# The first 512 rows of a seven-product matmul: the second half of k as seven products instead of plain ones

## The chip, the cores and the metric

The kernel runs on one core of a Trainium2 chip. The metric is the device time of one execution in microseconds, and the median of several runs is compared. A profile of one execution gives the busy times of the engines: PE does matmuls, DVE and ACT do elementwise work, POOL and SP issue transfers (POOL those that turn fp32 into fp16 on the way, SP plain ones).

## The reference

```python
def setup_inputs():
    m, k, n = 4096, 4096, 4096
    return {
        "a": np.random.randn(m, k).astype(np.float32),
        "b": np.random.randn(k, n).astype(np.float32),
        "bias": np.random.randn(n).astype(np.float32),
    }

def reference(a: np.ndarray, b: np.ndarray, bias: np.ndarray) -> np.ndarray:
    return np.tanh(np.matmul(a, b) + bias)
```

## The kernel before

**Arithmetic.** a and b are turned to fp16 as they are loaded, and sums are kept in fp32 banks of 128 x 512 (there are eight). The columns of the output come in four chunks of 1024 (c = 0 to 3), each two banks wide. Rows come in pairs of 128-row blocks. For a pair and a chunk, a is seen as a 2 x 2 matrix of blocks (a11, a12, a21, a22: upper or lower row block, first or second of the two sets of k, 16 steps of 128 each) and b likewise. Seven products P1 to P7 take the place of eight (Strassen's scheme in Winograd's form): P1 = a11 b11, P2 = a12 b21, P7 = s3 t3, P6 = s2 t2, P5 = s1 t1, P3 = s4 b22, P4 = a22 t4, with the left sums s1 = a21 + a22, s2 = s1 - a11, s3 = a11 - a21, s4 = a12 - s2 and the right sums t1 = b12 - b11, t2 = b22 - t1, t3 = b22 - b12 (put over b12), t4 = b21 - t2. DVE makes these sums. One such product of one pair is 16 matmuls of 128 x 128 by 128 x 512, one per step of k. Two pairs are worked together and called a duo. Some products are done a second time in the same manner, on quarters ("fine", line 856 and `fine_product`, line 840).

**Work of one duo.** `work` (line 946) emits a product and what follows it. Two pairs have four kinds of banks, D, Z, I and C (line 854): P1 and P2 add in D, which is finished as the upper left output; after P1, Z gets a copy of D, and P6 adds to it; I takes P7, and its copy p7 is added to Z (`lift`) and, after P5, to C (`after_p5`, line 1025), which gives the lower right output; C begins as Z plus the difference of the biases (`after_p6`, line 1001), takes P5 and then P3 (upper right); P4 adds to Z (lower left). `run_duo` (line 1044) sets the order P1, P2, then P7, P6, P7, P6, P5, P5, then P3, P4, P4, and P3 of the second pair inside the next duo. When P3 is reached, s4 is made, over s2.

**The first stage** (lines 1946 to 2144) is another one. The rows 0 to 1023 (row blocks 0 to 7; `g0` are 0 to 3, `g1` are 4 to 7) by the first 1024 columns are done by plain matmuls, 32 steps of k each, while b's columns and these rows still arrive. 24 matmuls on zeros come first, ahead of any data (line 1965). The eight banks can hold four row blocks, so partial sums go out to fp32 buffers ("spill", by ACT) and are taken up again (by DVE): k's first part of g0, its first part of g1, the rest of g0's first half, g1 to the end, and at last g0's second half (line 2143: 128 matmuls). Each `finish` is tanh on ACT and a store on SP. The row blocks of a come by POOL (`land`, line 2002) and are transposed by DVE into 16 tiles `aq[m, h]` (row block m, h the set of k); the second half of k comes last, one row block at a time. Then `firsts` makes s1 and s2 of the pairs 0 and 1 for later, and stores (`keep`, line 594 does the transfer) put a11, a12, a22, s2 into scratch memory, since later chunks of columns need them again.

**After it**, the six duos of rows 1024 to 4095 do the first 1024 columns by seven products (line 2207), loading their rows as `nat` tiles by POOL; then come the other columns (`wide_pass` and the two passes, line 1572 and the fine products), with pieces of a fetched from scratch.

**What sets the order.** Every operation is put to a planner (`Plan`, line 159) with a duration, the buffers that it reads and writes, and its bytes. `rank` works out due times backwards from the end; `schedule` simulates engines, transfers and the places of the chip's memory (51, line 28) and emits the instructions of each engine in the order of that simulation. A big buffer takes one place, an "out" buffer half of one. A transfer waits until its buffer has a place. `soft` brings a due time near that of what comes before it, `after` adds an operation that must precede; that is an order in the plan and no wait on the chip, unless a buffer is shared. Lines that the change touches besides: `load_bias` (line 913) and `store` and `finish` (lines 484 and 491), `product` (line 825), whose matmuls read the whole of a left tile as far as the planner knows.

The lines that set the end of the first stage:

```python
    for m, j in swapped:
        down(4 + m, j, 2 * T - TB, 2 * T, stop=True)
        finish(mb(m, j), 4 + m, j * NB)
        take_up(m, j, k0)
    for m, j in swapped:
        down(m, j, T, 2 * T, stop=True)
        finish(mb(m, j), m, j * NB)
```

Of the kernel before, what the change touches and what calls it, by code (L numbers as in the profile page):

```python
# [18 lines left out]
G = 2  # L19
WARM = 24  # L20
fp32 = mybir.dt.float32
# [137 lines left out]
class Plan:  # L159
# [14 lines left out]
    def add(self, eng, dur, emit, reads=(), writes=(), nbytes=0, hw=True, soft=None, early=0.0, lead=0.0, reach=1e9, after=None, long=False):  # L174
# [6 lines left out]
        if nbytes:  # L181
            kind = ("POOL", "LONG")[long] if not hw else "out" if soft is not None else "in"
            rate, wait = RATES[self.open][kind]
            op.flow, op.wait = nbytes / (rate * SPEED), wait + SLACK
            op.share = SHARES[self.open][long]
            op.kind = 0 if soft is None else 2 if writes else 1
# [222 lines left out]
def kernel(  # L409
# [73 lines left out]

    def store(o, row, col, n):
        add(
            "SP", 0.34,
            lambda: nc.sync.dma_start(out=out[ds(row * P, P), ds(col, n)], in_=o[ALL]),
            (o,), (), nbytes=P * n * 4, soft=1.0,
        )

    def finish(src, row, col):

        o = new("o", [P, NB], fp32, "out")
        act(NB, lambda: nc.scalar.activation(o[ALL], src[ALL], TANH), (src,), (o,), soft=2.0)  # L494
        store(o, row, col, NB)

# [328 lines left out]
    def product(bank, left, right, t0, nt, start=False, shift=0):  # L825

        for k in range(t0, t0 + nt, TB):
            rb = right[k // TB]

            def emit(k=k, rb=rb):  # L830
                for t in range(TB):
                    nc.tensor.matmul(  # L832
                        bank[ALL], left_tile(left, k + t + shift), rb.tile(t),
                        start=start and k == t0 and t == 0, stop=k + t == t0 + nt - 1,
                        skip_group_check=True,
                    )

            add("PE", TB * 0.2158, emit, ((left, left.atoms), *rb.deps()), (bank,))

# [73 lines left out]
    def load_bias(c, after=None):  # L913
        k = {}
        k["b1"] = new("bias", [P, 2, NB], fp32, atoms=2)
        src = bias[ds(c * NCW, NCW)]
        add(
            "SP", 0.34,
# [3 lines left out]
            ),  # L922
            (), (k["b1"],), nbytes=P * NCW * 4, after=after,
        )
# [18 lines left out]
    class Duo:  # L943
        pass

    def work(duo, name, s, part=None, last=True):
# [48 lines left out]
    def after_p1(d, s, part):  # L995
        if d.x == 0:
            src, atom = (d.k["b1"], 0) if part != 1 else (d.box[s], 0)
# [1119 lines left out]
    for m, j in rows4:  # L2117
        down(4 + m, j, 0, TB, True)
    across(g1, TB, TP - 2)
    for m, j in rows4:  # L2120
        down(4 + m, j, TP - 2, TP, stop=True)
        put_aside(4 + m, j)
        take_up(m, j)
    k0 = load_bias(0, plan.last_pe)
    for m, j in rows4:
        down(m, j, TB, TP)
    across(g0, TP, T - 2)
    for m, j in rows4:
        down(m, j, T - 2, T, stop=True)
        if j == 0:  # L2130
            new_spill(m)
        put_aside(m, j)
        take_up(4 + m, j, k0)
    for m, j in rows4:
        down(4 + m, j, TP, T)
# [9 lines left out]
    firsts = {}  # L2145
    for p in FIRST:
        s = {f"a{r + 1}{h + 1}": aq[2 * p + r, h] for r in range(2) for h in range(2)}
        asum(s, "s1", "a21", "a22", ADD, soft=2.0)
        asum(s, "s2", "s1", "a11", SUB, over="s1", soft=2.0)
        firsts[p] = s  # L2150
        if not KEEP_AT[p]:
            keep(p, s)
    finish_bias(k0)
    for blk in range(4):
        bsums(bop, blk)

    plan.open = 1
    stored |= early if TWO == 1 else set(range(NP))  # L2160
    k, before, held = k0, None, None
    for c in range(NC):
# [44 lines left out]
        for i, pairs in enumerate(duos):  # L2207
# [28 lines left out]
            for p in FIRST if c == 0 else ():  # L2236
                if KEEP_AT[p] == i + 1:
                    keep(p, firsts[p], after=plan.last_pe)
    def place_tile(buf):
# [44 lines left out]
```

## Time and profile before

| what | value |
|---|---|
| time, median of 3 runs | 1432.6 us (1432.56 to 1432.8) |
| time of the profiled execution | 1433.78 us |
| its span, first to last instruction | 1432.1 us |
| bytes moved by DMA | 399.19 MB |
| granted PE clock, mean | 1.000 |
| plain matmuls of the first stage (line 2049) | 512, from 9.80 us on |

In the rows of a timeline the columns are start and duration in us, engine, line, operation, output <- inputs, count, and in brackets the idle time ahead of it and what ended it. PEld is the loading of weights for PE, POOLq and SPq are the issue of transfers. A name like a or s is that of a buffer without its number; `parts` is a shared place of smaller buffers. In a view of waits the columns are total, times and longest in us. In a view of groups they are count, busy us, mean ns of one, and idle time before. In the DMA view a queue has packets, MB and a share (q0 is POOL's, q1 SP's), and a transfer has its count, KB and median us from issue to landing.

### The profile page before, as it was taken

Reading aid. Unit: us, or ns where it says so; the run is one execution under the profiler, and the core shown is the slowest. Engines: PE = TensorE matmul, PEld = TensorE weight load, DVE = VectorE, ACT = ScalarE, POOL = GpSimd, SP = SyncE. Lnnn points to the kernel's source line nnn. Section 1 sums busy time; section 2 is a strip of 40 time slices with the busy share of each in tenths; the row PEclk is TensorE's granted clock in tenths of the full one; section 3 lists DMA queues with packets and bytes.
Section 4 is the critical chain, followed back from the end, with each engine's and each line's share of the span. In section 5 each row is a group of like instructions: output and inputs, shape, how many; then the busy total and the mean of one; then the engine's idle time right before and its main releaser. Section 6 shows DMA issues by size and latency. Waiting matters only on the chain.

```text
span 1432.1 us, 22563 instructions
## 1 busy us (share of the span) xinstructions
PE 1422.2 (99%) x8408; PEld 822.2 (57%) x8408; DVE 1078.1 (75%) x1594; ACT 392.8 (27%) x746; POOL 325.3 (23%) x613
## 2 busy tenths in 40 slices
PE   9999999999999999999999999999999999999998
PEld 4444555555644444444444444444447888888887
DVE  3359968767985376796568787988798689997876
ACT  3111212221333333311111133233233332244433
POOL 8764332334452341100111130000130300000000
PEclk9999999999999999999999999999999999999999
DMA  9999998899999899997899799899999987788883
GB/s 188 178 236 286 251 293 196 222 240 221 274 276 316 235 274 302 280 358 290 265 291 294 270 294 389 341 367 344 334 335 354 271 248 265 250 297 286 304 301 134
DMA packets 167486, 399.19 MB, mean 279 GB/s; under 512 B 25425, under 2 KB 44369, under 8 KB 167377
## 3 DMA queue, kind: packets, MB, share of 16 engines
q1 hardware_dynamic: 104400, 318.03, 61.2%
q0 software_dynamic: 62976, 79.73, 33.4%
q8 instruction: 66, 1.08, 0.3%
q14 instruction: 44, 0.35, 0.1%
HBM read 327.68 MB, written 149.68 MB: 333 GB/s over the span
## 4 chain that ended last, share of the span: by engine, by line
PE 76%; DMA 2%; DVE 1%; POOL 0%; issue 0%; ACT 0%; SPq 0%; DVEq 0%
PE ps L1572 45%; PE ps L847 25%; PE ps L832 6%; DMA nat<-in_a_dram 1%; DMA xa<-a 1%; DMA s<-a 1%; DVE a L473 0%; POOL nat L530 0%; DVE s L473 0%; DVE a L506 0%; DVE u L473 0%; ACT parts L1370 0%; DVE ys L473 0%; DVE parts L473 0%; DVE za L684 0%
## 5 line engine op out<-in xcount | busy, mean ns | idle before, releaser
L759 POOL DMA_DIRECT2D b<-in_b_dram x320 | 169.7, 535 | 607.7 <-DMA out_dram<-u 163.6
L476 ACT COPY ps<-ps 128x256 f32<-128x256 f32 (+1 forms) x216 | 100.8, 467 | 443.0 <-PE ps L1572 306.0
L530 POOL DMA_DIRECT2D nat<-in_a_dram x224 | 118.5, 533 | 208.8 <-DMA nat<-in_a_dram 51.6
L473 DVE TENSOR_TENSOR u<-ps,u 128x512 f32<-128x512 f32 x160 | 106.1, 686 | 26.2 <-PE ps L1572 25.1
L473 DVE TENSOR_TENSOR parts<-ps,parts 128x512 f32<-128x512 f32 (+1 forms) x129 | 72.6, 563 | 67.2 <-PE ps L1572 40.0
L832 PEld LDWEIGHTS <-a 128*128 128x128 f16 x704 | 68.8, 98 | 81.9 <-issue 2.4
L473 DVE TENSOR_TENSOR ps<-ps,parts 128x256 f32<-128x256 f32 (+1 forms) x151 | 82.7, 552 | 39.4 <-PE ps L1572 22.0
L2049 PE MATMUL ps<-b,o 128*128 128x512 f16 x512 | 111.3, 379 | 0.1
L476 ACT COPY parts<-ps 128x256 f32<-128x256 f32 (+1 forms) x151 | 69.0, 461 | 135.9 <-DVE ps L473 45.6
L1572 PE MATMUL ps<-b,zs 128*128 128x512 f16 x448 | 105.8, 379 | 0.0
L1572 PEld LDWEIGHTS <-ya 128*128 128x128 f16 x624 | 61.1, 98 | 73.6
L506 DVE STREAM_TRANSPOSE a<-nat 128x512 uint32<-128x512 uint32 x112 | 73.2, 690 | 20.8 <-DMA nat<-in_a_dram 17.4
L832 PE MATMUL ps<-b,a 128*128 128x512 f16 x384 | 84.7, 379 | 2.1 <-DVE parts L473 2.1
L1572 PEld LDWEIGHTS <-zs 128*128 128x128 f16 x512 | 50.1, 98 | 60.2
L1572 PEld LDWEIGHTS <-xa 128*128 128x128 f16 x512 | 50.1, 98 | 60.2
L2049 PEld LDWEIGHTS <-o 128*128 128x128 f16 x512 | 49.8, 98 | 60.3 <-ACT o L2094 0.5
L494 ACT ACTIVATE parts<-ps 128x512 f32<-128x512 f32 x52 | 31.0, 597 | 162.4 <-PE ps L832 98.1
L1572 PE MATMUL ps<-b,za 128*128 128x512 f16 x320 | 75.6, 379 | 0.0
L473 DVE TENSOR_TENSOR b<-b,b 128x2048 f16<-128x2048 f16 (+2 forms) x76 | 68.0, 910 | 10.1 <-DMA b<-in_b_dram 9.5
L832 PE MATMUL ps<-t,a 128*128 128x512 f16 x320 | 72.3, 379 | 0.0
L1572 PEld LDWEIGHTS <-za 128*128 128x128 f16 x384 | 37.6, 98 | 45.3
L847 PEld LDWEIGHTS <-ya 128*128 128x128 f16 x592 | 57.9, 98 | 7.1
(163 smaller groups left out, 2560.1 us busy)
## 6 DMA issues: line engine op xcount, KB each, us to landing
b<-in_b_dram POOLq DMA_DIRECT2D x320, 128.0 KB, 8.0
ya<-a SPq DMA_DIRECT2D x70, 512.0 KB, 7.2
xa<-a SPq DMA_DIRECT2D x70, 512.0 KB, 7.2
u<-U SPq DMA_DIRECT2D x62, 512.0 KB, 6.6
nat<-in_a_dram POOLq DMA_DIRECT2D x224, 128.0 KB, 8.0
U<-u SPq DMA_DIRECT2D x48, 512.0 KB, 6.9
ys<-s SPq DMA_DIRECT2D x46, 512.0 KB, 5.0
xs<-s SPq DMA_DIRECT2D x46, 512.0 KB, 5.6
```

The lines of the kernel that those rows point to most:

```text
L473: dve(n, lambda: nc.vector.tensor_tensor(out=o(), in0=x(), in1=y(), op=op), reads, writes, wide, **kw)
L476: act(n, lambda: nc.scalar.copy(o(), x()), reads, writes, **kw)
L494: act(NB, lambda: nc.scalar.activation(o[ALL], src[ALL], TANH), (src,), (o,), soft=2.0)
L506: nc.vector.transpose(dst[ALL].rearrange("P t m -> P (t m)").bitcast(pair32).rearrange("P (U m) -> P U m", m=P)[:, ds(t0 // 2, nu), ds(row ...
L530: nc.gpsimd.dma_start(out=tl[(ds(q * QP, QP), *key)], in_=src)
L759: nc.gpsimd.dma_start(out=dst.rearrange("p t j n -> p t (j n)") if j is None else dst, in_=src)
L832: nc.tensor.matmul(bank[ALL], left_tile(left, k + t + shift), rb.tile(t), start=start and k == t0 and t == 0, stop=k + t == t0 + nt - 1, s ...
L847: nc.tensor.matmul(bank[ALL, HALF[half]], left_tile(buf, at_ * TP + i * TB + t), rb.tile(t), start=False, stop=i == 1 and t == TB - 1, ski ...
L1572: nc.tensor.matmul(bank[ALL, cols], left_tile(buf, at_ * TP + i * TB + t), rb.tile(t, half), start=start and not (i or t), stop=i == 1 and ...
L2049: nc.tensor.matmul(bank[ALL], left_tile(left, t), rb.tile(tb), start=start, stop=stop, skip_group_check=True,)
```

## The change

The first 512 rows keep plain matmuls only for the first half of k (`CLASSIC` = 16 steps). Their plain sums U = [u11 u12; u21 u22] (upper and lower row block, left and right bank) stay in the spill buffers, with the bias added. The second half of k is then done as a duo of its own by `run_duo`, each product over 8 steps, 14 products. The plain sums are fed in so that each output receives its own: D starts as u11 (an ACT copy) and Z is copied from it, I starts as u22's part less u12 (DVE), C gets e = u12 - u11 after P6, and Z gets one more sum at the lift. The left sums s1, s2, s3, s4 are made in halves of k, so that the first half need not wait for the second.

Beside that: s4 goes over a12 instead of s2 in all later duos of these columns (`S4_OVER`); the bias load now follows a DVE memset of its buffer that is ordered behind a matmul, and so waits on the chip; the stores of rows 512 to 1023 are put behind the store of row block 3's second tile (`behind`), and that store is pulled forward; the warm-up has 18 matmuls; the right sums are made for the blocks 1, 2, 3, 0 in place of 0 to 3; stores to scratch of the pairs 0 and 1 have other due times.

```diff
-WARM = 24
+WARM = 18
+CLASSIC = 16
+LATE_STORES = 2
+SLACK_OPEN = 0.8
+S4_OVER = 'a12'
-WARM_TIME = 7.6
+WARM_TIME = 6.7
...
+            rows_of = left.atoms if t0 == 0 else (k // TB,) if len(left.atoms) == 4 else (k // TP,)
-            add("PE", TB * 0.2158, emit, ((left, left.atoms), *rb.deps()), (bank,))
+            add("PE", TB * 0.2158, emit, ((left, rows_of), *rb.deps()), (bank,))
...
+        if after:
+            dve(NH, lambda: nc.vector.memset(k["b1"][ALL, 0, HI], 0.0), (), (k["b1"],), after=after)
...
         if name == "P3" and "s4" not in a_:
-            asum(a_, "s4", "a12", "s2", SUB, over=None if d.stays else "s2")
+            if d.sums:
+                d.last_sum(a_)
+            else:
+                asum(a_, "s4", "a12", "s2", SUB, over=None if d.stays else S4_OVER)
...
+        if d.sums:
+            t0, nt, start = CLASSIC // 2, T - CLASSIC // 2, False
...
+        elif d.sums:
+            e = d.sums[s]
+            tt(at(C[s]), at(Z[s]), at(e), ADD, NB, (Z[s], e), (C[s],))
...
+            if d.sums:
+                low = spill[d.pairs[s] * 2 + 1]
+                tt(at(Z[s]), at(Z[s]), at(low, ALL, 0), ADD, NB, (Z[s], (low, (0,))), (Z[s],))
...
     for m, j in rows4:
-        down(m, j, T - 2, T, stop=True)
-        if j == 0:
-            new_spill(m)
+        down(m, j, T - 2 if CLASSIC == T else TB, CLASSIC, stop=True)
         put_aside(m, j)
         take_up(4 + m, j, k0)
...
+    for m in g0:
+        tt(at(spill[m]), at(spill[m]), at(k0["b1"]), ADD, 2 * NB, (spill[m], k0["b1"]), (spill[m],))
+    first_duo = Duo()
+    d = first_duo
+    d.sums = []
+    for s in range(2):
+        up, low = spill[2 * s], spill[2 * s + 1]
+        e = new("e", [P, NB], fp32, "out")
+        tt(at(e), at(up, ALL, 1), at(up, ALL, 0), SUB, NB, (up,), (e,))
+        tt(at(low, ALL, 0), at(low, ALL, 0), at(low, ALL, 1), SUB, NB, (low,), ((low, (0,)),))
+        tt(at(low, ALL, 0), at(low, ALL, 0), at(e), ADD, NB, ((low, (0,)), e), ((low, (0,)),))
+        d.sums.append(e)
+    behind = None
+    if LATE_STORES:
+        m = 2 * LATE_STORES - 1
+        early_row = {"a22": aq[m, 1]}
+        keep(LATE_STORES - 1, early_row, ("a22",), soft=1.0)
+        behind = plan.ops[-1]
     for m, j in swapped:
         down(4 + m, j, 2 * T - TB, 2 * T, stop=True)
-        finish(mb(m, j), 4 + m, j * NB)
-        take_up(m, j, k0)
-    for m, j in swapped:
-        down(m, j, T, 2 * T, stop=True)
-        finish(mb(m, j), m, j * NB)
+        finish(mb(m, j), 4 + m, j * NB, behind)
+    for s in range(2):
+        copy(at(D[s]), at(spill[2 * s], ALL, 0), NB, ((spill[2 * s], (0,)),), (D[s],))
+    for s in range(2):
+        up, low = spill[2 * s], spill[2 * s + 1]
+        tt(at(I[s]), at(low, ALL, 1), at(up, ALL, 1), SUB, NB, ((low, (1,)), (up, (1,))), (I[s],))
+    finish_bias(k0)
+    for blk in (1, 2, 3, 0):
+        bsums(bop, blk)
...
+    for p in FIRST:
+        half_sum(s, "s1", "a21", "a22", ADD)
+        half_sum(s, "s3", "a11", "a21", SUB, over="a21")
+        half_sum(s, "s2", "s1", "a11", SUB)
...
+    d.c, d.k, d.bop, d.pairs = 0, k0, bop, list(FIRST)
+    d.x, d.next, d.put = 0, STEEP[0][0], ()
+    before = run_duo(d, None)
```

More of the change, by code (lines that the diff above doesn't have):

```diff
@@ L183, in add @@
             rate, wait = RATES[self.open][kind]
-            op.flow, op.wait = nbytes / (rate * SPEED), wait + SLACK
+            op.flow, op.wait = nbytes / (rate * SPEED), wait + (SLACK if self.open else SLACK_OPEN)
             op.share = SHARES[self.open][long]
@@ L482, with store @@
     ALL = slice(None)
-    def store(o, row, col, n):
+    def store(o, row, col, n, after=None):
         add(
@@ L943 @@
     class Duo:
-        pass
+        sums = None
     def work(duo, name, s, part=None, last=True):
@@ L995, in after_p1 @@
     def after_p1(d, s, part):
-        if d.x == 0:
+        if d.x == 0 and not d.sums:
             src, atom = (d.k["b1"], 0) if part != 1 else (d.box[s], 0)
@@ new lines, with half_sum, atoms @@
+    for s in range(2):
[6 more added lines that the diff above has]
+        bsums(bop, blk)
+    def half_sum(s, name, x, y, op, over=None, halves=(0, 1)):
+        x, y = s[x], s[y]
+        if name not in s:
+            s[name] = s[over] if over else new(name, [P, T, P], atoms=2)
+        def atoms(v, h):
+            return (h,) if len(v.atoms) == 2 else (2 * h, 2 * h + 1)
+        for h in halves:
+            key = ALL, ds(h * TP, TP)
+            tt(
+                at(s[name], *key), at(x, *key), at(y, *key), op, TP * P,
+                ((x, atoms(x, h)), (y, atoms(y, h))), ((s[name], atoms(s[name], h)),), wide=False,
+            )
@@ L2145, with last_sum @@
+    def last_sum(s):
+        half_sum(s, "s4", "a12", "s2", SUB, over="s3", halves=(1,) if CLASSIC == T else (0, 1))
     firsts = {}
+    d.a, d.last_sum = [], last_sum
     for p in FIRST:
         s = {f"a{r + 1}{h + 1}": aq[2 * p + r, h] for r in range(2) for h in range(2)}
-        asum(s, "s1", "a21", "a22", ADD, soft=2.0)
-        asum(s, "s2", "s1", "a11", SUB, over="s1", soft=2.0)
+        half_sum(s, "s1", "a21", "a22", ADD)
+        half_sum(s, "s3", "a11", "a21", SUB, over="a21")
+        half_sum(s, "s2", "s1", "a11", SUB)
@@ L2150 @@
         firsts[p] = s
+        d.a.append(s)
         if not KEEP_AT[p]:
[L2152 to L2155, printed above, removed]
+            keep(p, s, [n for n in BASIS if n != "a22" or p != LATE_STORES - 1], soft=3.0)
+    d.c, d.k, d.bop, d.pairs = 0, k0, bop, list(FIRST)
+    d.x, d.next, d.put = 0, STEEP[0][0], ()
+    d.parts = d.last = d.stays = False
+    before = run_duo(d, None)
     plan.open = 1
     stored |= early if TWO == 1 else set(range(NP))
-    k, before, held = k0, None, None
+    k, held = k0, None
@@ L2237 @@
                 if KEEP_AT[p] == i + 1:
-                    keep(p, firsts[p], after=plan.last_pe)
+                    keep(p, firsts[p], [n for n in BASIS if n != "a22" or p != LATE_STORES - 1], after=plan.last_pe, soft=3.0)
     def place_tile(buf):
```

21 lines of the change are left out of this document (12 added, 9 removed).

## The prediction

> **What bounds the kernel now.** I read the page first, then the view of waits for PE, PE's timeline and the chain of waits.
>
> ```profile
> span 1432.1 us, 22563 instructions
> PE 1422.2 (99%) x8408; PEld 822.2 (57%) x8408; DVE 1078.1 (75%) x1594; ACT 392.8 (27%) x746; POOL 325.3 (23%) x613
> ```
>
> ```profile
> PE ps L832 <- DVE parts L473: 2.1, 1, 2.1
> PE ps L847 <- DVE a L473: 1.7, 1, 1.7
> ...
> PE ps L847 <- ACT ps L476: 0.4, 1, 0.4
> ```
>
> PE is busy in 1422.2 of 1432.1 us, and in the whole run it stands still for another engine only three times (in the columns: total, times, longest), together 4.2 us. So a matmul that goes is worth its own time, a wait that goes is worth its own, and nothing else can pay.
>
> ```profile
> 11.18 110.11 PE L2049 MATMUL ps<-b,o 128*128 128x512 f16 x508
> 121.12 13.98 PE L832 MATMUL ps<-b,a 128*128 128x512 f16 x64
> ...
> 141.84 3.62 PE L832 MATMUL ps<-b,s 128*128 128x512 f16 x16
> ```
>
> The first stage runs without a gap. One matmul ends 0.38 us after its start, so the second row gives (13.98 - 0.38) / 63 = 0.216 us from one to the next.
>
> ```profile
> 409.53 189.95 PE ps L1572 x880
> ...
> 599.76 1.35 POOL nat L530 x3
> ...
> 637.58 440.47 PE ps L1572 x2040
> ```
>
> Where the chain leaves PE, at 599.5 us, POOL takes up right behind a PE instruction that freed a place, so that detour moves with PE: what is won before 600 us should arrive at the end.
>
> **The change part by part.**
>
> **A, the products.** The last 128 plain matmuls (512 rows, 1024 columns, 16 steps of k) become 14 products of 8 matmuls, 112. Sixteen go: 16 x 0.216 = **-3.5 us**, on PE's own path.
>
> **B, the start.** Six of 24 warm-up matmuls go, and the bias load no longer stands first on SP's queue.
>
> ```profile
> 1.40 7.63 PE L1968 MATMUL warm<-zeros 128*128 128x512 f16 x24 [1.40 <-DVE zeros L1962]
> ```
>
> ```profile
> 9.35 0.26 PEld L2088 LDWEIGHTS <-first 128*128 128x128 f16 x4 [0.24 <-DMA first<-in_a_dram]
> ...
> 10.86 0.27 PEld L2088 LDWEIGHTS <-first 128*128 128x128 f16 x4 [0.28 <-DMA first<-in_a_dram]
> ```
>
> ```profile
> 6.12 0.77 POOL L1975 DMA_DIRECT2D first<-in_a_dram  x1
> ```
>
> ```profile
> DMA to landing us min/median/max: 4.3/4.8/5.0
> ```
>
> The warm-up ends later than the first tile, but the second and the fourth tile of a's first columns are waited for, and the fourth was issued at 6.12 and landed 4.8 us on, at 10.9. Six matmuls at 0.216 are 1.3 us, and that is the upper end. As the loads hold PE back anyway, the gain is what a queue without the bias brings the fourth tile: from nothing to 10.86 - (6.12 + 4.3) = 0.4. I take **-0.2**. The same bias load now falls among loads that are late in the stage; that price is in D.
>
> **C, s4 in a12's place.** This touches every later duo of the first 1024 columns.
>
> ```profile
> 234.46 6.55 SPq L594 DMA_DIRECT2D s<-a  x3
> ```
>
> ```profile
> 250.45 1.23 DVE L473 TENSOR_TENSOR a<-a,a 128x2048 f16<-128x2048 f16 x1 [4.55 <-DMA s<-a]
> 251.59 0.68 DVE L473 TENSOR_TENSOR parts<-ps,parts 128x512 f32<-128x512 f32 x1
> ...
> 272.53 1.30 DVE L506 STREAM_TRANSPOSE a<-nat 128x512 uint32<-128x512 uint32 x2 [2.73 <-DMA nat<-in_a_dram]
> ...
> 279.75 1.23 DVE L473 TENSOR_TENSOR a<-a,a 128x2048 f16<-128x2048 f16 x1
> ```
>
> ```profile
> 252.33 3.61 PE L832 MATMUL ps<-b,a 128*128 128x512 f16 x16 [2.11 <-DVE parts L473]
> ...
> 281.04 1.05 PE L847 MATMUL ps<-b,a 128*128 128x256 f16 x8 [1.71 <-DVE a L473]
> ```
>
> ```profile
> 254.78 4.20 POOL L530 DMA_DIRECT2D nat<-in_a_dram  x8 [9.62 <-DVE parts L473]
> ```
>
> The reader is to see one cause behind two of the three waits. At 245.9 DVE comes to s4 = a12 - s2, which goes over s2, and s2 is still being stored to scratch (issued from 234.46 on). DVE's queue is in order, so for 4.55 us everything behind stands too: first the sum that empties bank C, for which PE waits 2.11 us, then the op whose end frees a place for POOL's next eight loads of a. Those are late, DVE waits for them at 272.53, and PE at 281.04 waits 1.71 for the DVE op that follows. With s4 over a12, whose store is earlier, there is nothing to wait for: 2.11 + 1.71 = **-3.8 us**. Ends: 0 (another store takes its place) and -3.8.
>
> **D, the new junction.** P1 of the first duo would start at 121.12 - 128 x 0.216 = 93.5, less B 93.3. Products are half as long, 1.73 us. What must be there by then:
>
> ```profile
> 88.42 2.52 POOL L530 DMA_DIRECT2D land<-in_a_dram  x4 [0.52 <-DMA land<-in_a_dram]
> ...
> 127.66 0.53 POOL L530 DMA_DIRECT2D nat<-in_a_dram  x1 [0.66 <-DMA nat<-in_a_dram]
> ```
>
> ```profile
> 88.28 0.70 DVE L473 TENSOR_TENSOR ps<-spill,bias 128x512 f32<-128x512 f32 x1 [26.00 <-ACT parts L494]
> ...
> 101.27 1.30 DVE L506 STREAM_TRANSPOSE o<-land 128x512 uint32<-128x512 uint32 x2
> ```
>
> ```profile
> q0 software_dynamic: 1871, 2.38, 111.8%
> ...
> land<-in_a_dram POOLq DMA_DIRECT2D x12, 128.0 KB, 5.4
> ```
>
> ```profile
> q0 software_dynamic: 1324, 1.21, 82.2%
> ```
>
> ```profile
> q0 software_dynamic: 1418, 2.32, 61.9%
> ...
> nat<-in_a_dram POOLq DMA_DIRECT2D x18, 128.0 KB, 9.0
> ```
>
> The three q0 rows are POOL's bytes in 75 to 88, 88 to 97 and 110 to 130 us: 183, 134 and 116 KB/us. The drop at 88 comes with the stores of rows 512 to 1023. Now these stores stand on SP behind the store of a row block of a that lands among the last, so until then POOL keeps 183: 9 x (183 - 134) = 0.44 MB earlier, 3.8 us at 116. Against this the bias (0.5 MB) now falls into the stage: 0.5 / 0.183 = 2.8 us at worst, nothing if it shares. The last row block (issued from 88.42 to 90.94) then lands at 90.94 + 5.4 = 96.3, transposed 1.3 later, against 101.9 before. P1 and P2 want rows 0 and 2, and the due times put those first; rows 1 and 3 are wanted from P7 on, at 93.3 + 32 x 0.216 = 100.2. So the loads of this stage should do. The next duo's last load is issued at 127.66, lands 9.0 later, and needs two transposes (1.3) and a sum (1.2): 139.2, where P7 of its second half started at 141.84 and now would at 138.2. It is 1.0 late if its loads do not come earlier, and on time if a third of those 3.8 us stays.
>
> ```profile
> L473 DVE TENSOR_TENSOR ps<-spill,bias 128x512 f32<-128x512 f32 x16 | 10.4, 684 | 28.4 <-ACT parts L494 26.0 <-ACT spill L476 2.4
> ...
> L473 DVE TENSOR_TENSOR t<-b 128x1024 f16<-128x1024 f16 x8 | 5.1, 686 | 0.0
> ...
> L473 DVE TENSOR_TENSOR s<-o,o 128x2048 f16<-128x2048 f16 x2 | 2.4, 1210 | 0.0
> ```
>
> DVE's work: the bias on four spills (8 x 0.68 = 5.5, no row has the whole width), six sums of halves (4.1), bank I (1.4), eight sums behind P6, P7, P5 (5.5), 16 half sums of a (16 x 0.64 = 10.2); gone are eight sums that took up rows 0 to 511 (5.5) and four whole sums (4.8). Net +16.4 us. Of it the spills (9.6) and the lower half sums (3.8) need nothing later than 62 us and lie in the 26.0 us in which DVE stood idle; cover gone, they are 13.4 us in front of P7. The rest, 3 us, is in a stretch where DVE has no pause. There a product behind a DVE sum has 1.73 us where it had 3.45: own 0.68 plus one 1.21 us sum ahead is 1.9, with a transpose too 2.6. Three places have such a turn (P6 to P5, P5 to P3, P7 to P4), 0.2 to 0.9 each. I take 0.5 each: **+1.5 us**; ends 0 and 6.9 (below). The ACT copies added (six) lie on an engine busy in 27% of the span.
>
> The Trainium skill speaks here (DMA: Bandwidth & Descriptors, section Queues, rings and completion order): each engine goes round robin, packet by packet, between the queue rows that have work. By that rule a store held back costs the loads nothing later, since a longer row takes no larger share, and the 3.8 us stay; the sum is as here. Were it shared by waiting bytes instead, they would be given back by 110 us, and D would be 2.5, the time 1428.1. The drop from 183 to 134 agrees with sharing by turns, but does not show what a longer row does.
>
> **E, the rest.** Every place is laid out anew behind the first stage. PE waits 0.4 us there, so nothing is to be won: 0 to +3, I take **+0.5**.
>
> **Sum:** -3.5 - 0.2 - 3.8 + 1.5 + 0.5 = -5.5. The profiled run took 1433.8 us, of which 1432.1 are the span; the median of the runs is 1432.6, 1.2 less than that run. The three become 1428.3, 1426.6 and **1427.1**.
>
> **Rivals.**
>
> *All clean:* A, B, C without D and E, -7.5: **1425.1**. For it: DVE's idle 26 us, the loads' 3.8 us. Against: turns of 1.73 us on an engine without a pause.
>
> *The operands are late:* rows 2's block stays last, as in the rows above, and is transposed at 101.27 plus 0.65 for its first half, 101.9; P1 of the second half wants it at 95.0. PE waits 6.9: **1432.0**. For it: DMA is full until then. Against: due times and stores held back.
>
> *The change does not do what it says:* s4 waits for a12's store, or o = C + p7 is late for another reason. C is 0: **1430.9**. Against: a12's store is issued with the row, s2's only after all sums.
>
> *Slower, by places:* s2 used to carry s4 to the end; now a12's place stays to the end of P3 and s2's until its store has landed.
>
> ```profile
> POOL nat L530 <- DVE a L506: 20.1, 3, 10.0
> ```
>
> ```profile
> 219.69 10.52 PE L832 MATMUL ps<-b,a 128*128 128x512 f16 x48
> ...
> 259.24 1.04 PE L847 MATMUL ps<-b,a 128*128 128x256 f16 x8
> ```
>
> ```profile
> 234.02 4.20 POOL L530 DMA_DIRECT2D nat<-in_a_dram  x8 [6.13 <-PE ps L847]
> ```
>
> P2 ends at 230.0 and let go of a12; two places are now held until about 250.4, when s2's store had landed. POOL waits for places already, three times behind transposes alone. If the eight loads of 234.02 had to start at 250.45, they would land 9.0 us later, and with a transpose (0.65) and four half sums (2.6) the fine P1 would start at 262.7 instead of 259.24: 3.4 late. With C lost and three such duos, -3.7 + 10.2: **1439.1**. It decides from 1.3 us a duo on. Against: places are shared, and two of the kernel's 51 are at stake.
>
> **Numbers.** Forecast 1427.1 (1425.6 to 1429.7): 0.50. All clean: 0.13. Operands late, 1432.0: 0.14. C missing, 1430.9: 0.09. Slower by places: 0.14. About 0.2% (2.9 us) is what a measurement of this kernel tells from no change: faster is below 1429.7, slower above 1435.5. Faster 0.50 + 0.13 + 0.02 (the lower part of the case without C) = 0.65; same 0.21; slower 0.14. The range leaves out half of the clean case's tail below 1424.6 (B at its 0.4 and more) and the case by places: 1424.6 to 1434.0.
>
> **What would show it.** A: 112 matmuls at the line of the products between the last plain one and the next duo. B: the first plain matmul near 9.6. C: no DVE wait for a store of s near 250, and none of PE at 252 and 281. D: PE's waits at the products' line between 93 and 142. E: no PE wait behind 282 that is not there now. The forecast is wrong if PE stands more than 4 us in D's stretch, or if POOL's loads of a in the next duos start later relative to PE than now.

## The result, and the profile after

| | before | after |
|---|---|---|
| median, same chip (21 runs each) | 1433.78 us | 1431.41 us |
| lowest to highest | 1432.29 to 1437.43 | 1427.62 to 1434.46 |
| profiled execution, its span | 1433.78, 1432.1 us | 1431.41, 1429.1 us |
| mean granted PE clock of that execution | 1.000 | 0.998 |
| runs at a mean granted clock of 1.000 (full speed) | (26 of 35 in a second set) | 6 of 21 |

The ratio is 0.9983, interval 0.9975 to 0.9990: 2.4 us faster (1.4 to 3.6), where 5.5 were forecast. The direction held and the time lies in the range; less than half of the gain arrived.

The head of the page of the kernel after:

```profile
span 1429.1 us, 22558 instructions
...
PE 1417.6 (99%) x8386; PEld 820.4 (57%) x8386; DVE 1090.6 (76%) x1617; ACT 395.6 (28%) x752; POOL 325.4 (23%) x613
```

PE has 4.6 us less work. That is 1.1 more than the 16 matmuls of step A: six warm-up matmuls went too, and the start gave some back. The span shrank by 3.0 only. The view of waits for PE (total, times, longest) shows where the rest is:

```profile
PE ps L852 <- DVE a L477: 2.8, 1, 2.8
PE tp L2106 <- DMA first<-in_a_dram: 2.7, 1, 2.7
...
PE ps L852 <- DVE ps L477: 0.3, 1, 0.3
PE ps L852 <- ACT ps L480: 0.2, 1, 0.2
```

Before there were waits of 2.1 and 1.7 at two places of the later duos. Now there is one of 2.8, and a new one of 2.7 at the start, ahead of the transposes of a's second tile. PE's timeline of the kernel after (its lines stand 4 to 18 further down: 836 is the line of the products, 852 of the fine ones, 2067 of the plain matmuls) puts them in their places:

```profile
1.40 5.43 PE L1986 MATMUL warm<-zeros 128*128 128x512 f16 x18 [1.40 <-DVE zeros L1980]
6.67 0.39 PE L2106 MATMUL tp<-ident,first 128*128 128x128 f16 x4
9.78 0.41 PE L2106 MATMUL tp<-ident,first 128*128 128x128 f16 x4 [2.72 <-DMA first<-in_a_dram]
...
11.82 83.49 PE L2067 MATMUL ps<-b,o 128*128 128x512 f16 x380
95.14 8.80 PE L836 MATMUL ps<-b,o 128*128 128x512 f16 x40
...
133.13 3.62 PE L836 MATMUL ps<-b,s 128*128 128x512 f16 x16
...
248.44 3.62 PE L836 MATMUL ps<-b,a 128*128 128x512 f16 x16
...
278.24 1.05 PE L852 MATMUL ps<-b,a 128*128 128x256 f16 x8 [2.80 <-DVE a L477]
...
401.29 1.89 PE L1590 MATMUL ps<-b,a 128*128 128x512 f16 x8
```

The last row is the first matmul of the next columns; it stands among the last of these duos. Before, that row was:

```profile
404.19 1.89 PE L1572 MATMUL ps<-b,a 128*128 128x512 f16 x8
```

**The junction.** From the first product at 95.14 to the next duo's P7 at 133.13 are 37.99 us. Before, the last plain matmuls began at 121.12 - 128 x 0.216 = 93.49, and that P7 at 134.94, two products (6.91) ahead of the 141.84 of the prediction: 41.45. Step A is there whole, -3.5, and PE stands nowhere between 95 and 278.

**The start.** The first product starts at 95.14 and not at the 93.3 forecast. The windows of the kernel after, and PE's weight load for the fourth tile, show why. The columns of a window are its length, the busy time of PE, PEld, DVE, ACT and POOL (each with its count), the granted clock, DMA share and GB/s:

```profile
8.00:10.00 2.00, 0.23 (x4) 0.23 (x5) 0.00 (x0) 0.00 (x0) 1.64 (x3) 1.00 1.66 183
10.00:12.00 2.00, 2.00 (x17) 1.05 (x15) 0.79 (x2) 0.76 (x2) 1.51 (x3) 0.76 1.15 194
12.00:14.00 2.00, 2.00 (x7) 0.59 (x5) 0.00 (x0) 0.75 (x2) 1.93 (x4) 0.50 1.31 182
14.00:16.00 2.00, 2.00 (x10) 0.89 (x9) 0.00 (x0) 0.00 (x0) 1.65 (x3) 0.88 1.39 176
```

```profile
11.40 0.35 PEld L2106 LDWEIGHTS <-first 128*128 128x128 f16 x4 [0.54 <-DMA first<-in_a_dram]
```

PE was idle for 2.72 us behind the shorter warm-up, and the clock then fell to 0.76, 0.50 and 0.88 for two microseconds each: (0.24 + 0.50 + 0.12) x 2 = 1.7 us of clock. The first product comes 95.14 - 93.49 = 1.65 later than the same point before, in two parts. The matmuls behind the fourth tile start at 11.82 where they started at 11.18, 0.64 later: that tile was waited for until 11.40, later than the 10.86 before, although the bias load had left the head of SP's queue. The 380 matmuls from there to the first product take 83.32 us where they took 82.31, 1.01 longer, and the clock from 12 us on, (0.50 + 0.12) x 2 = 1.24, covers that.

**The wait that moved.** The wait ahead of the product at 252.33 is gone: its successor at 248.44 follows without a gap. But the wait ahead of the fine P1 grew from 1.71 to 2.80. POOL's timeline of the kernel after, and DVE's, beside those in the prediction:

```profile
251.54 4.20 POOL L534 DMA_DIRECT2D nat<-in_a_dram  x8 [8.72 <-DMA out_dram<-parts]
```

```profile
247.89 0.69 DVE L477 TENSOR_TENSOR ya<-a 128x1024 f16<-128x1024 f16 x1 [1.38 <-DMA s<-a]
...
269.76 1.30 DVE L510 STREAM_TRANSPOSE a<-nat 128x512 uint32<-128x512 uint32 x2 [3.16 <-DMA nat<-in_a_dram]
...
276.95 1.23 DVE L477 TENSOR_TENSOR a<-a,a 128x2048 f16<-128x2048 f16 x1
```

The eight loads wait for a place as they did (8.72 us, before 9.62), only that the place now comes free when a store of the output has landed, and no longer with a DVE op. DVE, too, still waits for a store of an s (1.38, before 4.55), but PE no longer stands behind it. The eight loads start 254.78 - 251.54 = 3.24 us earlier, where PE's product (252.33 to 248.44) starts 3.89 earlier: relative to PE the loads are *later*, which the prediction had named as the sign that it is wrong. From them it goes on: transposes wait 3.16 for their loads at 269.76, and the sum of 276.95, four sums and two more transposes later, is the one that PE waits for. That operand lets PE go at 278.24, 2.80 earlier than the 281.04 of before, PE arrives 3.89 earlier, and the difference is the 1.09 by which the wait grew. From P7 of the next duo to the next columns are 401.29 - 133.13 = 268.16 us where 404.19 - 134.94 = 269.25 were: 1.09 less, and not 3.8.

### The profile page after: what moved, and what is told of

Its sections match the earlier page's. It is cut to its first block, busy times and chain, and to the rows that moved or that the text cites. A ratio compares the mean times of both kernels' runs of the same rounds, so it can differ in the third digit from the quotient of the medians.

```text
span 1429.1 us, 22558 instructions
## 1 busy us (share of the span) xinstructions
PE 1417.6 (99%) x8386; PEld 820.4 (57%) x8386; DVE 1090.6 (76%) x1617; ACT 395.6 (28%) x752; POOL 325.4 (23%) x613
## 4 chain that ended last, share of the span: by engine, by line
PE 78%; DMA 1%; DVE 1%; ACT 0%; issue 0%; SPq 0%; DVEq 0%
PE ps L1590 47%; PE ps L852 25%; PE ps L836 6%; DMA xa<-a 1%; DVE parts L477 0%; ACT parts L1388 0%; DVE za L688 0%; DVE s L477 0%; DVE a L477 0%; DVE ps L477 0%; DVE t L477 0%; DVE cs L477 0%; DVE a L510 0%; ACT ps L480 0%; SPq L491 0%
## 5 line engine op out<-in xcount | busy, mean ns | idle before, releaser
L480 ACT COPY ps<-ps 128x512 f32<-128x512 f32 (+1 forms) x218 | 101.9, 468 | 445.7 <-PE ps L1590 308.9
L477 DVE TENSOR_TENSOR parts<-ps,parts 128x256 f32<-128x256 f32 (+1 forms) x131 | 73.8, 564 | 75.0 <-PE ps L1590 39.6
L836 PEld LDWEIGHTS <-a 128*128 128x128 f16 x768 | 75.1, 98 | 86.9 <-DVE a L477 0.2
L836 PE MATMUL ps<-b,a 128*128 128x512 f16 x448 | 99.1, 379 | 0.0
L2067 PE MATMUL ps<-b,o 128*128 128x512 f16 x384 | 84.9, 384 | 0.0
L2067 PEld LDWEIGHTS <-o 128*128 128x128 f16 x384 | 37.8, 99 | 45.6 <-issue 1.1
```

The lines of the kernel that those rows point to most:

```text
L477: dve(n, lambda: nc.vector.tensor_tensor(out=o(), in0=x(), in1=y(), op=op), reads, writes, wide, **kw)
L480: act(n, lambda: nc.scalar.copy(o(), x()), reads, writes, **kw)
L836: nc.tensor.matmul(bank[ALL], left_tile(left, k + t + shift), rb.tile(t), start=start and k == t0 and t == 0, stop=k + t == t0 + nt - 1, s ...
L2067: nc.tensor.matmul(bank[ALL], left_tile(left, t), rb.tile(tb), start=start, stop=stop, skip_group_check=True,)
```

## The experiments

The theory before the first of them: the first 1024 columns of the later duos run at the pace of loads (and of the places that these need). A wait taken away there comes back further on, and a pause long enough lets PE's clock fall behind it. The main rival: DVE, which has 12.5 us more work (1090.6 after 1078.1), sets the new waits. A second one holds that the loss is all at the start. Ratios are to the kernel before on the same chip.

**Warm-up.** After with the longer warm-up (the planner's figure for it, 6.7 us, left), with a still longer one, and before with the shorter one:

```diff
-WARM = 18        e1          -WARM = 18        e2          -WARM = 24        e3, before
+WARM = 24                    +WARM = 30                    +WARM = 18
```

> The changed kernel with 24 warm-up matmuls in place of 18, nothing else (the planner's figures stay, so every later instruction keeps its order). Theory 'clock': in the changed kernel PE stands for 2.7 us behind the short warm-up, the granted clock is then 0.76, 0.50 and 0.88 in the three stretches of 2 us from 10 to 16 us, and that costs about 1.1 us beside the 0.6 us later start. With 24 the pause falls to about 1.4 us, the clock stays 1.00 from 10 us on, and the products' first matmul comes near 94.0 in place of 95.14: span about 1427.9, ratio to before about 0.9972. Theory 'loads': the first tiles of a set the start in both, the clock's dip has another cause; the start of the products stays at 95.1 within 0.3 and the ratio stays 0.998.

> The changed kernel with 30 warm-up matmuls, so that they end at about 9.3 us, near the landing of the second tile of a. Theory 'clock': no pause above 0.6 us, clock 1.00 from 8 us on, the products' first matmul at 94.0 or up to 0.4 later, since transposes of the first tile now come behind the warm-up: like 24, ratio about 0.9972. Theory 'loads': as with 18, products at 95.1.

> The kernel before with 18 warm-up matmuls in place of 24, nothing else. Theory 'clock': the pause that the changed kernel has appears here too, PE's clock dips behind it, and the first stage ends 0.8 to 1.7 us later (first product at 122 to 122.9 in place of 121.12): ratio 1.0006 to 1.0012. Theory 'loads': nothing moves, first product at 121.1 within 0.3, ratio 1.000.

Measured: e1 1430.27 us, ratio 0.9974 (0.9962 to 0.9985); e2 1431.64, 0.9984 (0.9973 to 0.9994); e3 1432.72, 0.9992 (0.9983 to 1.0000). PE's timeline of e1, then that of e2 and its windows:

```profile
9.08 0.61 PE L2106 MATMUL tp<-ident,first 128*128 128x128 f16 x8
...
276.99 1.05 PE L852 MATMUL ps<-b,a 128*128 128x256 f16 x8 [2.69 <-DVE a L477]
```

```profile
279.66 1.36 PE L852 MATMUL ps<-b,a 128*128 128x256 f16 x8 [2.89 <-DVE a L477]
280.81 1.91 PE L852 MATMUL ps<-f1t,ys 128*128 128x256 f16 x8
282.52 1.60 PE L852 MATMUL ps<-b,zs 128*128 128x256 f16 x8
283.96 1.04 PE L852 MATMUL ps<-f2t,ys 128*128 128x256 f16 x8
```

```profile
278.00:280.00 2.00, 0.34 (x4) 0.31 (x5) 1.93 (x3) 0.00 (x0) 1.43 (x3) 1.00 0.98 261
280.00:282.00 2.00, 2.00 (x13) 1.45 (x11) 2.00 (x4) 0.36 (x1) 0.00 (x0) 0.56 0.81 160
282.00:284.00 2.00, 2.00 (x13) 1.43 (x12) 2.00 (x4) 0.00 (x0) 0.00 (x0) 0.58 1.05 205
284.00:286.00 2.00, 2.00 (x20) 1.70 (x18) 2.00 (x3) 0.47 (x2) 0.71 (x2) 1.00 0.81 302
```

e1 did as its theory of the clock expected at the start: its first product starts at 93.70 (near 94.0 was expected), 1.4 earlier than in the kernel after, with no pause and no dip at the start; the first matmul of the next columns comes at 400.05 (after 401.29, before 404.19). The interval of e1 overlaps that of the change, so the 1.1 us between the medians are not settled. e2 missed: its ratio was expected like e1's, but its warm-up lasts until 10.89, its first product comes at 95.35, and its clock dips at 280. What stays in e1 is the wait of 2.69, and e2's rows show what such a pause can do: eight fine matmuls that take 1.04 us take 1.91 behind it. Of e1's 12 runs, five show a mean clock of 1.000 (median 1427.4), seven less (median 1431.3): 3.9 us for the same program. The theory that all is lost at the start falls: e1 has no pause there, and most of its runs lose clock all the same; e3 has one of 2.40 us, and all its 12 runs stand at 1.000 and are no slower than before, as the rival of loads had it (its duos begin at 121.35, before at 121.12).

**s4 alone, and everything but s4.**

```diff
 e4, in before:  -asum(a_, "s4", "a12", "s2", SUB, over=None if d.stays else "s2")
                 +asum(a_, "s4", "a12", "s2", SUB, over=None if d.stays else "a12")
 e7, in after:   -S4_OVER = 'a12'
                 +S4_OVER = 's2'
```

> The kernel before with s4 over a12 instead of s2 in the duos of the first 1024 columns, nothing else. Theory 'wait moved': the 2.11 us in which PE stood at 250.2 goes, and the wait at 279.3 grows from 1.71 to about 2.8, since places are still freed late by s2's store and the loads behind start late: net -1.0 us, ratio 0.9993. Rival, the prediction's step C: both waits go, -3.8 us, ratio 0.9973. Rival 'places': two more places held cost loads elsewhere, +1 us or more.

> The changed kernel with s4 over s2 again, nothing else. Theory 'wait moved': PE waits near 250 for about 2 us, the wait near 278 falls to 1.7 or less; each is too short for the clock to fall, so although PE stands longer in sum, more runs stay at 1.000 and the median is within 1 us of the changed kernel's (ratio 0.9975 to 0.999). Rival, the prediction's step C: it gives back 3.8 us, ratio 1.001.

Measured: e4 1433.11 us, 0.9996 (0.9988 to 1.0004); e7 1435.22, 1.0007 (0.9998 to 1.0017). PE's timeline of e4, and of e7:

```profile
234.89 0.38 PE L847 MATMUL ps<-f2t,ys 128*128 128x256 f16 x2 [0.56 <-DVE f2t L473]
279.13 1.05 PE L847 MATMUL ps<-b,a 128*128 128x256 f16 x8 [0.53 <-DVE a L473]
374.86 1.05 PE L847 MATMUL ps<-b,a 128*128 128x256 f16 x8 [1.85 <-DVE a L473]
...
404.36 1.89 PE L1572 MATMUL ps<-b,a 128*128 128x512 f16 x8
```

```profile
157.09 5.03 PE L836 MATMUL ps<-b,s 128*128 128x512 f16 x16 [3.92 <-DVE s L477]
375.25 1.05 PE L852 MATMUL ps<-b,a 128*128 128x256 f16 x8 [1.91 <-DVE a L477]
...
404.75 1.89 PE L1590 MATMUL ps<-b,a 128*128 128x512 f16 x8
```

e4 is the failed step by itself. In the old kernel the edit does nearly all that was forecast of it at its own place: the wait at 252 is gone, and the one at 281 falls to 0.53 (it did not grow, as the theory had it). Nevertheless nothing that can be measured is won, since 1.85 us stand in the last duo, at 374.86, where there were none. PE's waits between 95 and 410 us add up to 2.9 after 3.8; in e3, whose duos are those of before, they add up to 3.2, so part of even this is the spread between executions. From the first product of these duos to the next columns e4 takes 404.36 - 121.60 = 282.76 us, the kernel before 283.07 and e3 283.02: 0.3 us is won of 3.8.

In the changed kernel the edit is needed all the same: without it the ratio is 0.24% higher, and the two intervals do not touch. Here the theory missed (0.9975 to 0.999), and the number of its rival, step C as forecast, came true (1.001), though by another wait: none returns near 250, but PE waits 3.92 us at 157.09, and the slow 16 matmuls (5.03 instead of 3.62) show the clock falling behind it. So the two gains cannot be priced one by one. From the end of the plain matmuls to the next columns the kernel before takes 404.19 - 93.49 = 310.70 us, e7 (step A without C) 404.75 - 94.30 = 310.45, and the kernel after 401.29 - 95.14 = 306.15. A alone brings 0.25 us to the end of this stage, C alone 0.3, both together 4.55. These are single executions, and e7's has the dip of the clock in it.

**The order of the left sums.** s3 first, then s2 = a22 - s3 and s1 = s2 + a11 over a11, which needs the fifth place of a pair later. e5 (with WARM = 24) and e6 (18) do so in all the later duos but the last, e10 in one duo, e11 in all with the last (both with WARM = 24):

```diff
             asum(s, "s3", "a11", "a21", SUB, over="a21")
...
-            asum(s, "s2", "s1", "a11", SUB, over="a11")
+            asum(s, "s2", "a22", "s3", SUB)
+            asum(s, "s1", "s2", "a11", ADD, over="a11")
```

> The changed kernel with 24 warm-up matmuls and, in the later duos of these columns, the left sums in another order: s3 = a11 - a21 first, then s2 = a22 - s3 and s1 = s2 + a11 behind P1, so that P7 waits for one sum instead of two and s1 needs no place of its own before. (The sums are the same in exact arithmetic, rounded in another order.) Theory 'pause': what keeps the gain back is PE's wait of 2.8 us near 278, whose end is the chain last load, transposes, s1, s3; it is long enough for the clock to fall behind it in some runs (3.9 us more in the seven runs of twelve with a mean clock below 1.000 than in the other five). Here the wait should fall to 1.6 or less, the mean clock be 1.000 in at least ten of twelve runs, the median 1426 to 1427.5, ratio 0.995 to 0.996. Rival 'loads set it': the wait only moves to another place of these duos, the sum of PE's waits between 200 and 410 us stays near 2.8, and the clock falls as often; ratio 0.9974.

> The same with the 18 warm-up matmuls of the changed kernel. If the pause behind the short warm-up costs by the clock, some runs are still below 1.000, and the median is 0.5 to 2 us over that with 24. If the start's pause is harmless, as in the kernel before with 18 (12 of 12 runs at 1.000), the two have the same median within 0.5.

> The changed kernel with 24 warm-up matmuls and s3 ahead of s2 and s1 in one duo alone, the one whose P7 is waited for near 278 (rows 2560 to 3071). If that wait is the chain behind the last load, it falls by the 1.2 us of one sum, to 1.6 or less, the clock stays at 1.000 in more than half of the runs, median 1426.5 to 1428.5. If the loads set the stage, the wait comes back in one of the two later duos (as it did at 371 with the order changed in all), 3 us or more in sum, median 1430 or more.

> The changed kernel with 24 warm-up matmuls and s3 ahead of s2 and s1 in every later duo, the last one too. Against the run that left the last one out (PE waited 3.7 us at 371, all eleven runs below a clock of 1.000): the wait at 371 falls by one sum, to about 2.4, if nothing else moves; runs at 1.000 come back (a quarter or more), median 1429 to 1431.

Measured: e5 1432.37 us, 0.9996 (0.9987 to 1.0004); e6 1432.23, 0.9993 (0.9984 to 1.0002); e10 1432.47, 0.9986 (0.9976 to 0.9996); e11 1427.34, 0.9956 (0.9943 to 0.9968). PE's timelines of e5, e10 and e11:

```profile
371.20 1.89 PE L853 MATMUL ps<-b,a 128*128 128x256 f16 x8 [3.66 <-DVE a L477]
```

```profile
284.10 1.03 PE L862 MATMUL ps<-f4t,a 128*128 128x256 f16 x8 [2.04 <-DVE ps L478]
371.38 1.05 PE L862 MATMUL ps<-b,a 128*128 128x256 f16 x8 [1.42 <-DVE a L478]
```

```profile
235.39 1.03 PE L857 MATMUL ps<-f4t,a 128*128 128x256 f16 x8 [0.71 <-DVE ps L477]
368.19 1.05 PE L857 MATMUL ps<-b,a 128*128 128x256 f16 x8 [0.18 <-DVE a L477]
```

Three times the wait near 278 went and stood further on, as the rival "loads set it" had expected and the theory had not; e6's 3.58 us is at 371.62, as e5's. e5 is even slower than e1, whose interval it does not touch. The medians of e5 and e6 lie 0.1 apart, so the shorter warm-up costs nothing that shows there. Only with the new order in all duos does the wait stay away, and e11 is faster than was expected of it (1429 to 1431). e11 is the version that beats both kernels: by 0.44% (0.32 to 0.57) the one before, and its interval lies below that of the change. Against e1, which has its warm-up, the intervals still overlap a little (0.9943 to 0.9968 and 0.9962 to 0.9985), so how much of this is the order alone is not settled. Its first matmul of the next columns comes at 398.05, 3.2 us ahead of the kernel after. Which of the places freed earlier does it is not shown: the planner lays out all of them anew with each edit.

**The stores held back.**

```diff
 e8, in after:   -LATE_STORES = 2
                 +LATE_STORES = 0
```

> The changed kernel without the hold on the stores of rows 512 to 1023. The prediction's step D has it that held stores bring the last loads forward: without it POOL's bytes between 88 and 97 us fall from 1.41 to about 1.2 MB, row block 3 is transposed about 2 to 3 us later than 101.8, P7 of the second pair (slack about 0.9 us) waits 1 to 2 us near 105, and the time is 1 to 2 us longer than the changed kernel's. Rival: the loads come as before, no wait of PE between 95 and 117 us, same time.

Measured: 1433.71 us, 1.0002 (0.9990 to 1.0014). PE's timeline of e8, and the POOL queue of the DMA view in 88 to 97 us, of the kernel after and then of e8 (packets, MB, share):

```profile
105.91 1.90 PE L836 MATMUL ps<-b,o 128*128 128x512 f16 x8 [1.73 <-DVE o L477]
112.18 1.89 PE L836 MATMUL ps<-t,s 128*128 128x512 f16 x8 [0.92 <-DVE ps L477]
123.59 3.63 PE L836 MATMUL ps<-b,a 128*128 128x512 f16 x16 [0.89 <-DVE a L510]
```

```profile
q0 software_dynamic: 1550, 1.41, 100.8%
```

```profile
q0 software_dynamic: 1254, 1.14, 81.5%
```

With the stores let go, POOL moves 1.14 MB for 1.41 in these 9 us, and PE waits 3.5 us in the junction, where it did not wait at all; the wait near 105 and the lost 2 us are what was expected. (The edit also lets go the one store that was pulled forward.) In 110 to 130 us it is 2.17 MB for 2.57, so up to there nothing was given back. On what a held store costs later, the rule of turns that the prediction took from the Trainium skill (DMA: Bandwidth & Descriptors, Queues, rings and completion order) agrees with these two pairs of numbers.

**No output stores in the stage, and more products.**

```diff
 e9, in after, WARM = 24:    def store(o, row, col, n, after=None):
                            +    if row >= 8 and col < NCW:
                            +        return
 e12, in after, WARM = 24:  -CLASSIC = 16
                            +CLASSIC = 8
```

> The changed kernel with 24 warm-up matmuls and without the output stores of rows 1024 to 4095 in the first 1024 columns (that part of the output is left unwritten; all sums are still made). It takes 48 transfers of 256 KB off SP's queue and gives their places back at once. Theory 'loads set the stage': PE's waits between 140 and 410 us (2.8 in the changed kernel, 3.1 in the run with 24) come from loads that queue for places and for the transfer engines beside those stores; here their sum falls below 1.0, no pause is longer than 1 us, the mean clock is 1.000 in nearly all runs, and the time is that of 24 warm-up matmuls without the waits, 1424 to 1426 (ratio 0.993 to 0.995). Rival 'DVE': the waits are DVE's own queue of sums; the waits stay above 2, ratio 0.9975.

> The changed kernel with 24 warm-up matmuls and plain products for the first 8 of 32 steps of k only, so that 24 of 32 steps go by seven products: another 8 x 14 - ... in numbers 64 plain and 168 in products, 232 matmuls where the change has 128 + 112 = 240: 8 fewer, 1.7 us. Step A alone: the first duo after the stage starts 1.7 us earlier, ratio 0.9962. Theory 'loads set the stage': that 1.7 us is given back in waits before 410 us (sum 4.5 or more), the pause behind it is longer, the clock falls in more runs, ratio 0.9975 to 0.9990.

Measured: e9 1425.49 us, 0.9941 (0.9928 to 0.9955), without a wait of PE between 12 and 410 us and with all four runs at a clock of 1.000; e12 1439.33, 1.0037 (1.0024 to 1.0051). PE's timeline of e12:

```profile
58.04 30.41 PE L2067 MATMUL ps<-b,o 128*128 128x512 f16 x128 [5.93 <-DMA b<-in_b_dram]
...
94.11 11.34 PE L836 MATMUL ps<-b,o 128*128 128x512 f16 x44 [2.20 <-DVE o L510]
```

e9 leaves rows 1024 to 4095 of these columns unwritten. DVE's work stays as it is (1088.8 us after 1090.6), and with the stores every wait is gone, as was expected: the rival that DVE's own work sets them falls. Whether the stores matter by the bytes that they take from the loads or by the places that they hold until they have landed, e9 does not tell, as it takes away both. e12 has eight matmuls fewer than the change and takes 5.1 us more than before on its chip (1434.22): PE is done with what it has at 52.1 us, when b is not there yet, waits 5.93 until 58.04, and all five runs show a lowered clock. It was expected to give back its 1.7 us and lost far more: laid out like this, the first stage has no room for eight matmuls fewer.

**The clock and the longest pause.** All kernels, by the longest pause of PE behind the warm-up in the profile of each, and the runs whose mean clock was 1.000:

| kernel | longest pause, us | runs at 1.000 |
|---|---|---|
| e11, e9 | 0.7, 1.2 | 3 of 5 (the others 0.999 or above), 4 of 4 |
| e4, e8, e10 | 1.9, 2.0, 2.0 | 9 of 12, 3 of 10, 6 of 11 |
| before, e3 | 2.1, 2.4 | 26 of 35, 12 of 12 |
| e1, after, e2 | 2.7, 2.8, 2.9 | 5 of 12, 6 of 21, 3 of 12 |
| e6, e5, e7, e12 | 3.6, 3.7, 3.9, 5.9 | 1 of 11, 0 of 11, 0 of 11, 0 of 5 |

The pause is that of one execution, the counts are of all. It is an order, not a threshold: from 2.7 us on most runs lose clock, from 3.6 on nearly all. e8 with its 2.0 does not fit, and no run says why. The traces themselves overlap in the same way: in these profiles the clock dips behind pauses of 2.20 (e12, at 94), 2.72, 2.89 and each of 3.58 and more, and holds behind 2.40 (e3), 2.69 (e1) and the 2.80 at 278 of the kernel after.

## Why the prediction was right and wrong

In the spans the steps come to -3.5 + 1.65 - 1.0 - 0.2 = -3.0, where -5.5 stood.

- **A, the products: right.** -3.46 for -3.5, from the two stretches of 37.99 and 41.45.
- **B, the start: wrong in sign in the profiled run.** +1.65 (93.49 to 95.14) for -0.2, of which 1.01 stand behind the fourth tile, where the clock is low. "As the loads hold PE back anyway" was right; that the bias in front of them cost up to 0.4 was wrong, since without it the fourth tile came no earlier. The forecast took a shorter warm-up to be free and had no term for what a pause does to the clock. In the other runs with 18 warm-up matmuls the pause was 1.4 to 2.4 and no dip of this size followed: their first products start at 93.66 (e8), 94.06 (e6) and 94.30 (e7). So the start costs 0.2 to 1.7 in these profiles and gains in none.
- **C, s4 in a12's place: the step that failed.** "2.11 + 1.71 = -3.8" became -2.11 + 1.09 = -1.0. The reading "one cause behind two of the three waits" was right for the first of them and for the stall of DVE's queue, and in e4 the second shrinks with it. What failed is the rule that the prediction sets out from, "a wait that goes is worth its own", and with it the 1.71 counted as won: the chain that ends the wait at 278 begins with loads, and these wait for places and for the landing of stores, so whoever brings PE there sooner makes PE wait longer, at that point or further on. e4 shows it with this edit alone (0.3 us won in the stage for 3.8), e5, e6 and e10 show it with another cure, and e9 shows that the output stores have a part in that pace. e7 shows the other side: without this edit step A's 3.46 are lost again in waits and in the dip behind one of them. The terms of the sum were not independent.
- **D, the junction: better than forecast, and in part by luck.** 0 for +1.5. DVE's new work went into the pause that the prediction named. The windows of DVE's pause, before and then after (the third pair of numbers is DVE's), and DVE's transposes of the row block that comes last, after:

```profile
62.00:75.00 13.00, 13.00 (x62) 5.92 (x61) 0.29 (x1) 0.00 (x0) 9.39 (x18) 1.00 1.07 178
75.00:88.00 13.00, 13.00 (x62) 5.89 (x61) 0.00 (x0) 0.34 (x1) 9.78 (x19) 1.00 1.12 185
```

```profile
62.00:75.00 13.00, 13.00 (x62) 5.88 (x61) 10.51 (x16) 0.00 (x0) 9.43 (x18) 1.00 1.05 172
75.00:88.00 13.00, 13.00 (x62) 5.88 (x60) 7.58 (x12) 0.00 (x0) 9.77 (x20) 1.00 1.12 193
```

```profile
101.83 1.30 DVE L510 STREAM_TRANSPOSE o<-land 128x512 uint32<-128x512 uint32 x2
```

  DVE now works 18.1 of these 26 us. The 3.8 us from the stores held back did not show as earlier loads: 1.41 MB where 1.21 had been is 0.20 more, not 0.44, and the transposes of the last row block begin at 101.83, where it was 101.27 before and where the prediction had the block land at 96.3. The bias, issued at 29.71, took 0.52 MB of the transfers between 12 and 75 us, and POOL moved 11.27 MB there for 11.63; with the held stores it moved 3.90 for 3.59 from 75 to 97 and so won most of that back. Without them PE waits 3.5 (e8). That PE stands nowhere although these loads came no sooner was no part of the sum. The rival of late operands stood one edit away.
- **E, the rest: small, as forecast**, -0.2 for +0.5; it is what the other steps leave of the 3.0.
- **The rival "slower by places"** came nearest to the mechanism: places set when loads start. It had the price wrong, 10.2 us for a wait that grew by 1.1.

Beside this sum stands the clock. The profiled run has its dip at the start; e1 has no pause there, and still seven of its 12 runs lose 3.9 us. The only pause of its profile over 0.4 us is the one of 2.69, and e2's windows show the dip behind the same wait. That the same happens there in e1's lower runs is inferred, as only one execution of each kernel has a trace. Where it does not happen, e1 takes 1427.4 us against 1433.3 of the runs of before at 1.000, 5.9 less. That is about the size forecast, but it is another start and a choice of the better runs, and its wait of 2.69 is still there; it does not make the sum right.

What stays open: why the six runs of the change at 1.000 (median 1430.1) are still 2.6 above e1's, and why the planner's layout sends the wait to 278 in one kernel and to 371 in another.

## What to carry to other kernels

A wait in a stage that runs at the pace of loads is not worth its length: ask when the operand of the next such point arrives, and count only what both PE and the loads gain. When matmuls are saved there, watch the longest single pause and not only the sum of waits, because one pause of 2.7 us and more can lower the clock behind it, which was worth 1.7 us more in the windows of after, e2 and e7. Idle time of another engine ahead of a junction, and stores that can wait behind loads, were good cover for new work.

## What was not expected of the hardware

- PE's clock fell behind pauses well under 3.4 us: 2.72 (to 0.50 in the windows above), 2.89 (to 0.56 and 0.58, for about 4 us) and, in e12 at 94 us, 2.20 (to 0.52 and 0.62). The Trainium skill (TensorE: Matmul & The Clock Gate, section HAM oscillation — how this bites in real kernels) puts the bound at gaps of more than about 3.4 us; here the measurement decides, and the bound is lower. The same page (What's actually happening) says that the window in which activity is judged runs free. That pauses of 2.40, 2.69 and 2.80 were followed by no dip, and those of 2.20, 2.72 and 2.89 by one, agrees with it, though no trace here shows the window.
- The dips come in two sizes. Added up over windows of 2 us, (1 - clock) x 2, each of them is 1.7 us (after and e2 1.72, e7 1.70, e12 at 94 us 1.72) or 3.4 (e5 3.40, e6 3.42, e12 at 58 us 3.40). In e5 and e6 a part of the dip lies in the pause itself, where it costs nothing.
- The warm-up on zeros, which waits for nothing, takes a different time in each execution: 18 matmuls took 5.43, 5.49, 6.00 and 6.49 us in the profiles of after, e3, e8 and e7, 24 took 6.67 (e9) to 8.14 (e10). So the length of the pause behind it varies by chance, here from 1.4 (e6) to 2.7 with 18.
- Fewer bytes ahead of the loads did not make them land sooner: in 5 to 12 us POOL's loads moved 1.19 MB in the kernel after and 1.33 before, with the bias out of the way in the former.
